# A diffusion block on one core: attention ordered by pair, two token tiles and head, and the modulation moved to ScalarE and GpSimd

## The chip, the core and the metric

The kernel runs on one core of a Trainium2 chip. A core has five engines that run on their own instruction queues, each in order: TensorE (PE in the profile, with PEld for its weight loads), VectorE (DVE), ScalarE (ACT), GpSimd (POOL) and SyncE (SP), which here issues every DMA. Matmul results land in PSUM, which has eight banks; everything else lives in SBUF. The metric is the device time of one execution in microseconds (us), lower is better. Three runs of the kernel before took 1487.81, 1483.56 and 1487.60 us, so the median is 1487.6 us.

## The reference, cut to what matters

One transformer block over 1024 tokens (a grid of 16 rows by 64 columns) of width 1024, in fp32, with 256 context tokens that are only attended to. Sixteen heads of 64.

```python
sh1, sc1, g1, sh2, sc2, g2 = adaln(c, w_mod, b_mod)            # silu(c) @ w_mod + b_mod, cut in six
csh1, csc1, *_ = adaln(c_ctx, w_mod, b_mod)
h  = rms_norm(x, norm1)   * (1 + sc1)  + sh1                    # 1024 x 1024
hc = rms_norm(ctx, norm1) * (1 + csc1) + csh1                   #  256 x 1024
q, k = rms_norm(heads(h @ w_q), q_gain), rms_norm(heads(h @ w_k), k_gain)   # norm over the 64 of a head
v = heads(h @ w_v);  kc = rms_norm(heads(hc @ w_k), k_gain);  vc = heads(hc @ w_v)
# each token attends to a window of 8 x 16 tokens (with a relative bias) and to all 256 context tokens
p = softmax([q @ k_window / 8 + rpb, q @ kc / 8])
x = x + g1 * ((p @ [v_window, vc]) @ w_o)
a, g = split(modulate(rms_norm(x, norm2), sh2, sc2) @ w_up)     # 1024 x 2816 each
x = x + g2 * ((a * gelu(dwconv3(g))) @ w_down)
```

`rms_norm(t) = t / sqrt(mean(t*t) + 1e-6) * gain`.

## The kernel before

Tokens are cut into eight tiles of 128 (each is 16 rows by 8 columns of the grid), t = 0 to 7, and the context into two, t = 8 and 9; the order of work is 8, 9, 0, 1, ... 7 (`TORD`). A window touches only the neighbouring tiles, so tile t attends to tiles t-1, t, t+1 and to the context: 512 scores a row at the edges (t = 0 and 7) and 640 elsewhere. Every fp32 product is made of three fp32r matmuls: an operand is split in a high part (`wh`, `hth`: a rounded copy made on ACT) and a low part (`wl`, `htl`: a subtraction on DVE or POOL).

The program has four stages:

1. **The prologue.** Shift and scale of the first norm from `w_mod` (tiles `mraw`); then each token tile `xt` is loaded, normalised, transposed on TensorE (`pt`), modulated and split (`hth`, `htl`). The loop interleaves this with the projections of the first pair of heads: after transposing tile number i it makes projections up to tile number i - `AHEAD`.
2. **The attention of eight pairs of heads.** `qkv_gen(p)` is the generator of the projections of pair p: ten tiles, 24 matmuls each into a PSUM tile `pq` (two buffers). When a tile's matmuls are done it is taken out of PSUM: ACT squares q and k (`qsq`), DVE sums the squares (`qss`, `L323`), DVE scales the sums and adds epsilon (`L324`), POOL takes the power of -1/2 (`L325`), and DVE writes `q` (per head), `kn` and the low part of `v` (per head; ACT writes its high part). `pq` is free again only after the last of these. `k_stack` transposes `kn` (`kt`) into the keys `k`. The steps (p, h, t) are: `stage_a` transposes q (`qt`, split into `qh`, `ql`); `stage_b` makes the scores `s` (one PSUM buffer of two banks), DVE adds the bias and finds the row's extreme (`L410`, writes `p`), ACT takes the exponential (`L412`), DVE the reciprocal of the sum (`m`, `L413`), POOL multiplies by it (`L417`); two steps later `stage_c` transposes `p` (`pl`, `pc`) and splits it (`pt`); three steps later `stage_d` multiplies by `v` (`po`), adds the two halves (ACT `ot`, DVE `or`) and stores to `o_dram`. The steps run over the head's eight tiles, then the other head's. Between the stages `filler(6)`, `filler(5)` and `filler(5)` put 16 matmuls of the projections of the *next* pair into each step; at step (h = 0, t = 5) what is left of one pair is emitted at once and the next pair's generator is started. `build_bias` makes one head's bias on POOL from `rpb`, at the end of the head before.
   Beside it `mod_gen` computes the remaining four parts of the modulation on DVE: 16 blocks of eight loads `mr` (128 x 256 each, two buffers), each multiplied by a column of `cs` and added to `macc` (`L469`, `L471`), one or two loads per step.
3. **The output projection.** `wo_first` makes its first half (pairs 0 to 3) beside the last pair; the second half, the second norm and the operands of the next product follow.
4. **The feed-forward part** in a Winograd form (seven products of halves in place of eight), up and down. The diff leaves its code alone.

What sets the order on each engine: the program is written in one order, and a scheduler of the compiler places each instruction when its inputs and a free buffer are there, the earlier-written first. The resulting queue of each engine is fixed at build time; at run time an engine that waits at its head holds up all that is queued behind it.

## Time and profile before

| | before |
|---|---|
| runs (three), median | 1483.56 to 1487.81 us, 1487.6 us |
| span of the profiled execution | 1491.8 us, the only time shown of that execution |
| mean granted TensorE clock | 0.974 of full speed |
| TensorE busy, 0 to 100 us (prologue) | 68.6 of 100 us |
| TensorE busy, 100 to 600 us (attention) | 479.2 of 500 us, clock 0.98 |
| DVE / ACT / POOL busy, 100 to 600 us | 418.3 / 295.1 / 259.6 us |
| TensorE busy, 830 to 1180 us (up projection) | 349.1 of 350 us |

The span runs from the first to the last instruction of one execution under the profiler. It is 4.2 us above the median of the runs. A matmul's span contains its way through the array, so consecutive matmuls overlap: TensorE's busy share is not its share of the peak, and a stall shows only where the spans do not touch. A row of the grouped view reads: line, engine, operation, tile written and tiles read, shapes, count, then busy us, mean ns of one, and the idle time of the engine before them with what ended it.

### The profile page before, as it was taken

The page shows a single profiled execution, that of the slowest core. Times are in us where ns is not written, and L with a number is a line of the kernel's source. Part 1 is how long each engine was busy: PE and PEld are TensorE (multiplying, and loading weights), DVE is VectorE, ACT ScalarE, POOL GpSimd, SP SyncE. Part 2 cuts the span into 40 slices and gives each one's busy share as a digit, 9 for nine tenths or more (in the row PEclk, how much of TensorE's full clock was granted, in tenths as well). Part 3 has the DMA queues.
Part 4 walks back from the last instruction along what each step waited for, and adds up shares of the span by engine and source line. Part 5 has one row for each costly group of instructions (what it writes and reads, how often), then busy time and mean ns, then how long its engine had stood idle before and what let it go on. Part 6 is the DMA issues. An engine that isn't in the chain of part 4 may idle for free.

```text
span 1491.8 us, 22077 instructions
## 1 busy us (share of the span) xinstructions
PE 1386.5 (93%) x7396; PEld 1200.0 (80%) x7396; DVE 1208.1 (81%) x2392; ACT 738.1 (49%) x1601; POOL 805.7 (54%) x672
## 2 busy tenths in 40 slices
PE   6689999999999999999996999999999987898998
PEld 2589889898989899888885777888888865686887
DVE  6778878888888878866589889788877779988884
ACT  6575645555565656645465434344343334244541
POOL 1455544545454546744368545555545568474872
PEclk9899999999999999999997999999999998899999
DMA  9612221313131202262132132233332347433343
GB/s 315 161 37 60 64 87 55 92 51 103 49 101 45 77 14 73 69 152 76 50 129 99 64 108 101 96 106 106 107 106 99 106 137 286 155 100 127 110 131 105
DMA packets 84827, 153.27 MB, mean 103 GB/s; under 512 B 9945, under 2 KB 49001, under 8 KB 84713
## 3 DMA queue, kind: packets, MB, share of 16 engines
q1 hardware_dynamic: 84712, 151.86, 32.7%
q8 instruction: 58, 0.95, 0.3%
q14 instruction: 57, 0.46, 0.1%
HBM read 119.05 MB, written 32.78 MB: 102 GB/s over the span
## 4 chain that ended last, share of the span: by engine, by line
PE 60%; DVE 20%; DMA 7%; POOL 5%; issue 4%; ACT 3%; SPq 0%; DVEq 0%; POOLq 0%; ACTq 0%
PE pg L740 8%; PE pa L740 7%; PE sw L740 6%; PE pq L301 5%; PE pq L303 5%; PE pq L305 5%; DMA mr<-in_w_mod_dram 2%; DVE y L787 2%; DVE p L410 2%; POOL u L688 2%; PE s L398 2%; PE po L448 2%; PE po L449 2%; PE py L525 2%; PE py L526 2%
## 5 line engine op out<-in xcount | busy, mean ns | idle before, releaser
L688 POOL TENSOR_TENSOR u<-ur,u 128x512 fp32r<-128x512 f32 x154 | 231.9, 1519 | 176.8 <-ACT u L687 175.1
L417 POOL TENSOR_TENSOR p<-p,m 128x640 f32<-128x640 f32 (+1 forms) x128 | 157.3, 1230 | 157.0 <-DVE m L413 116.0
L301 PE MATMUL pq<-wh,hth 128*128 128x384 f32 (+1 forms) x640 | 219.7, 343 | 17.1 <-DVE kn L340 15.3
L305 PE MATMUL pq<-wh,htl 128*128 128x384 f32 (+1 forms) x640 | 215.2, 336 | 2.4 <-DVE htl L194 1.4
L303 PE MATMUL pq<-wl,hth 128*128 128x384 f32 (+1 forms) x640 | 215.0, 336 | 0.5 <-POOL wl L147 0.5
L687 ACT ACTIVATE u<-ur 128x512 fp32r<-128x512 f32 x154 | 93.9, 628 | 116.1 <-PE sw L740 45.4
L412 ACT ACTIVATE p<-p,m 128x640 f32<-128x640 f32 (+1 forms) x128 | 102.9, 804 | 84.3 <-DVE m L410 75.2
L301 PEld LDWEIGHTS pq<-wh,hth 128*128 128x128 f32 x640 | 124.8, 195 | 23.1 <-DVE kn L340 9.2
L325 POOL TENSOR_TENSOR qss<-qss,mhalf 128x4 f32<-128x4 f32 (+1 forms) x80 | 79.9, 999 | 97.0 <-DVE qss L324 82.8
L305 PEld LDWEIGHTS pq<-wh,htl 128*128 128x128 f32 x640 | 124.7, 195 | 3.2 <-DVE htl L194 3.2
L303 PEld LDWEIGHTS pq<-wl,hth 128*128 128x128 f32 x640 | 124.8, 195 | 1.6 <-issue 0.9
L787 DVE SCALAR_TENSOR_TENSOR y<-g,cw,y 128x896 f32<-128x896 f32 (+1 forms) x132 | 102.8, 842 | 19.2 <-ACT y L781 19.1
L449 PE MATMUL po<-pt,v 128*128 128x256 f32 x352 | 93.3, 293 | 2.1 <-DVE pt L437 2.1
L448 PE MATMUL po<-pt,v 128*128 128x256 f32 x352 | 93.8, 289 | 0.1
L895 ACT ACTIVATE db<-dr 128x512 fp32r<-128x512 f32 x77 | 47.4, 629 | 87.3 <-PE dx L911 55.7
L871 POOL TENSOR_TENSOR da<-da 128x512 fp32r<-128x512 f32 x44 | 74.9, 1725 | 27.4 <-ACT da L870 27.4
L896 POOL TENSOR_TENSOR db<-dr,db 128x512 fp32r<-128x512 f32 x44 | 64.9, 1494 | 45.6 <-ACT db L895 34.3
L410 DVE CUSTOM_DVE_ANT_0 p<-s,bias 128x640 f32<-128x640 f32 x96 | 78.3, 816 | 9.5 <-PE s L399 8.9
L436 ACT ACTIVATE pt<-pl 128x384 fp32r<-128x384 f32 (+1 forms) x128 | 58.0, 461 | 47.6 <-PE pl L429 46.6
L471 DVE SCALAR_TENSOR_TENSOR macc<-mr,cs,macc 128x256 f32<-128x256 f32 x112 | 65.0, 581 | 13.9 <-DMA mr<-in_w_mod_dram 13.0
L437 DVE TENSOR_TENSOR pt<-pl,pt 128x384 fp32r<-128x384 f32 (+1 forms) x128 | 65.4, 516 | 6.7 <-ACT pt L436 6.2
L449 PEld LDWEIGHTS po<-pt,v 128*128 128x128 f32 x352 | 66.6, 189 | 4.0 <-DVE pt L437 3.4
(258 smaller groups left out, 4184.3 us busy)
## 6 DMA issues: line engine op xcount, KB each, us to landing
ur<-in_w_up_dram SPq DMA_DIRECT2D x44, 512.0 KB
da<-act_dram SPq DMA_DIRECT2D x77, 256.0 KB
mr<-in_w_mod_dram SPq DMA_DIRECT2D x128, 128.0 KB
dr<-in_w_down_dram SPq DMA_DIRECT2D x22, 512.0 KB
wraw<-in_w_qkv_dram SPq DMA_DIRECT2D x56, 192.0 KB
mraw<-in_w_mod_dram SPq DMA_DIRECT2D x16, 512.0 KB
act_dram<-sa SPq DMA_DIRECT2D x11, 512.0 KB
act_dram<-y SPq DMA_DIRECT2D x11, 512.0 KB
```

Source lines behind the costliest of these rows:

```text
L301: PE.matmul(pq[:, c0:], hth[t][:, k, :], wh[:, c0:], start=(k == 0), stop=False)
L303: PE.matmul(pq[:, c0:], hth[t][:, k, :], wl[:, c0:], start=False, stop=False)
L305: PE.matmul(pq[:, c0:], htl[t][:, k, :], wh[:, c0:], start=False, stop=(k == KC - 1))
L410: DVE.tensor_tensor_reduce(out=dst, in0=src, in1=bb, scale=1.0, scalar=3e38, op0=ALU.add, op1=ALU.min, accum_out=m[:, 0:1])
L412: ACT.activation(w[:, :n], w[:, :n], AF.Exp, bias=m[:, 0:1], scale=-1.0, accum_out=m[:, 1:2])
L417: POOL.tensor_tensor(w[:, :n], w[:, :n], m[:, 2:3].broadcast_to([P, n]), ALU.mult)
L448: PE.matmul(po, v, th[:, j].rearrange("p a b -> p (a b)"), start=(m == 0), stop=False)
L449: PE.matmul(po, v, tl[:, j].rearrange("p a b -> p (a b)"), start=False, stop=(m == len(blks) - 1))
L687: ACT.activation(s[:, 0], r[op], AF.Copy)
L688: POOL.tensor_tensor(s[:, 1], r[op], f(s[:, 0]), ALU.subtract)
L740: PE.matmul(bank, a, b, start=(start and k == 0 and n == 0), stop=(k == 3 and n == 2), skip_group_check=True)
L787: DVE.scalar_tensor_tensor(o, i, w, o, ALU.mult, ALU.add)
```

## The change

The change rewrites the attention's order and some of its small operations:

- **Steps by pair, two tiles, head.** The steps become (p, u, h, i) with t = 2u + i: two tiles of the first head, the same two of the second, then the next two tiles. The last pair takes u in the order 0, 2, 1, 3.
- **One chain of projections.** `work()` strings the projections of all eight pairs and the first half of the output projection into one generator. A counter `done` of finished tiles is capped at what the step needs plus five (`LEAD`), and `need()` emits what is missing.
- **Both heads in one operation.** `v` (high and low part), `q` and the bias tile now hold both heads; the buffers go from 23 half tiles to 10 tiles for `v` (`VB`) and from 14 to 6 for `q` (`QB`). For the second head the scores lie with the context behind the window instead of in front, so that both biases share the block of zeros.
- **Epsilon as a 65th column.** The squares are scaled by 1/64 on ACT and a constant 65th column holds epsilon, so the sum is the mean plus epsilon and `L324` is gone.
- **Modulation on ACT and POOL.** `L469` and `L471` become an ACT multiplication of every `mr` (`L481`) and, for seven of eight, an addition on POOL (`L483`).
- `AHEAD` goes from 1 to 3; `ot` is gone (ACT writes `or`, DVE adds in place).

```diff
-AHEAD = 1
+AHEAD = 3
+QB, VB, LEAD = 6, 10, 5
...
+    sqc = sb.tile([P, 4, DH + 1], F32, name="sqc")
+    POOL.memset(sqc[:, :, DH:], EPS)
...
-            ACT.activation(sq[:, 4 - n:, :], pq[:, c0:2 * P].rearrange("p (h d) -> p h d", d=DH), AF.Square)
-            DVE.tensor_reduce(ss[:, 4 - n:], sq[:, 4 - n:, :], axis=AX.X, op=ALU.add)
-            DVE.tensor_scalar(ss[:, 4 - n:], ss[:, 4 - n:], 1.0 / DH, EPS, ALU.mult, ALU.add)
+            ACT.activation(sqc[:, 4 - n:, :DH], pq[:, c0:2 * P].rearrange("p (h d) -> p h d", d=DH), AF.Square,
+                           scale=DH ** -0.5)
+            DVE.tensor_reduce(ss[:, 4 - n:], sqc[:, 4 - n:, :], axis=AX.X, op=ALU.add)
             POOL.tensor_tensor(ss[:, 4 - n:], ss[:, 4 - n:], mhalf[:, 4 - n:], ALU.pow)
-            for h in range(2):
-                v = sb.tile([P, 2, DH], F32R, tag="v", bufs=23, name=f"v{p}_{h}_{t}")
-                pv = pq[:, 2 * P + h * DH:2 * P + (h + 1) * DH]
-                ACT.activation(v[:, 0, :], pv, AF.Copy)
-                DVE.tensor_tensor(v[:, 1, :], pv, f(v[:, 0, :]), ALU.subtract)
...
+            v = sb.tile([P, 2, 2, DH], F32R, tag="v", bufs=VB, name=f"v{p}_{t}")
+            pv = pq[:, 2 * P:].rearrange("p (h d) -> p h d", d=DH)
+            ACT.activation(v[:, :, 0, :], pv, AF.Copy)
+            DVE.tensor_tensor(v[:, :, 1, :], pv, f(v[:, :, 0, :]), ALU.subtract)
...
+                q = sb.tile([P, 2, 2, DH], F32, tag="q", bufs=QB, name=f"q{p}_{t}")
+                DVE.tensor_tensor(q, pq[:, :P].rearrange("p (h d) -> p h d", d=DH).unsqueeze(2)
+                                  .broadcast_to([P, 2, 2, DH]),
+                                  ss[:, :2].unsqueeze(2).unsqueeze(3).broadcast_to([P, 2, 2, DH]), ALU.mult)
...
+            done[0] += 1
...
-        ACT.activation(tmp[a:b], po[o:o + DH], AF.Copy)
-        DVE.tensor_tensor(res[a:b], po[a:b], tmp[a:b], ALU.add)
+        ACT.activation(res[a:b], po[o:o + DH], AF.Copy)
+        DVE.tensor_tensor(res[a:b], po[a:b], res[a:b], ALU.add)
...
-                    if k == 0:
-                        DVE.tensor_scalar(acc, raw, cs[:, k, 0:1], None, ALU.mult)
-                    else:
-                        DVE.scalar_tensor_tensor(acc, raw, cs[:, k, 0:1], acc, ALU.mult, ALU.add)
+                    ACT.activation(acc if k == 0 else raw, raw, AF.Copy, scale=cs[:, k, 0:1])
+                    if k:
+                        POOL.tensor_tensor(acc, acc, raw, ALU.add)
...
-    steps = [(p, h, t) for p in range(NPAIR) for h in range(2) for t in range(NB)]
-    steps[-NB:] = [(NPAIR - 1, 1, t) for t in LORD]
+    steps = [(p, h, 2 * u + i) for p in range(NPAIR) for u in ((0, 1, 2, 3) if p + 1 < NPAIR else (0, 2, 1, 3))
+             for h in range(2) for i in range(2)]
...
+    def work():
+        for p in range(NPAIR):
+            yield from qkv_gen(p)
+        yield from wo_first()
...
-        while n > 0:
+        while n > 0 and done[0] < cap[0]:
...
-            if h == 0 and t == 5:
-                filler(10 ** 6)
-                fill = qkv_gen(p + 1) if p + 1 < NPAIR else wo_first()
+            cap[0] = 10 ** 6 if p + 1 == NPAIR else NT * p + 2 + 2 * (t // 2) + LEAD
+            need(p, t)
...
-            if si % NB == NB - 1 and 2 * p + h + 1 < HEADS:
-                build_bias(2 * p + h + 1)
+            if p + 1 < NPAIR and t == NB - 1:
+                build_bias(2 * (p + 1) + h)
```

What that moves in the queues, at three places. In the rows, the first number in a name is the pair, then the head where the tile belongs to one head, then the token tile; the last is a buffer number.

First, SP's queue in the prologue, from the first `rpb` on. `wraw` are weights of pair 1, `xt4` to `xt7` the last token tiles, `mr2048_0` and on the loads of the modulation. Before:

```order
L366 DMA rpb0_1109<-in_rpb_t_dram 128x384
L136 DMA wraw1_2_1140<-in_w_qkv_dram 128x384
L136 DMA wraw1_3_1142<-in_w_qkv_dram 128x384
L168 DMA xt4_532<-in_x_dram 128x1x1024
L136 DMA wraw1_4_1144<-in_w_qkv_dram 128x384
L467 DMA mr2048_0_1187<-in_w_mod_dram 128x256
L467 DMA mr2048_1_1251<-in_w_mod_dram 128x256
L168 DMA xt5_601<-in_x_dram 128x1x1024
L366 DMA rpb1_1498<-in_rpb_t_dram 128x384
L467 DMA mr2048_2_1254<-in_w_mod_dram 128x256
```

Now:

```order
L374 DMA rpb0_974<-in_rpb_t_dram 128x384
L480 DMA mr2048_0_1007<-in_w_mod_dram 128x256
L480 DMA mr2048_1_1028<-in_w_mod_dram 128x256
L169 DMA xt4_491<-in_x_dram 128x1x1024
L137 DMA wraw1_2_1313<-in_w_qkv_dram 128x384
L137 DMA wraw1_3_1315<-in_w_qkv_dram 128x384
L137 DMA wraw1_4_1317<-in_w_qkv_dram 128x384
L169 DMA xt5_522<-in_x_dram 128x1x1024
L480 DMA mr2048_2_1032<-in_w_mod_dram 128x256
L374 DMA rpb1_981<-in_rpb_t_dram 128x384
L480 DMA mr2048_3_1055<-in_w_mod_dram 128x256
L169 DMA xt6_591<-in_x_dram 128x1x1024
```

Before, `xt6` stands behind ten loads `mr`; now it stands behind four, with `xt7` right after it. The first two `mr` move ahead of `xt4` and of three `wraw`.

Second, TensorE between pairs 3 and 4, from the first score of pair 4 (`s4_0_0`) on. Before, the last projection of pair 4 (`pq4_7`) lies around the score, and the transposes `pl4_0_0` of that step come 64 rows after it, with 11 more matmuls of `pq4_7` and all 24 of the next tile between:

```order
L301 MATMUL pq4_7_5706<-wh4_4_4636,hth7_108 128x384
L398 MATMUL s4_0_0_5481<-k4_0_4826,qh4_0_0_5421 128x256
L399 MATMUL s4_0_0_5481<-k4_0_4826,qh4_0_0_5421 128x256
L398 MATMUL s4_0_0_5481<-k4_0_4826,ql4_0_0_5422 128x256
L399 MATMUL s4_0_0_5481<-k4_0_4826,ql4_0_0_5422 128x256
L303 MATMUL pq4_7_5706<-wl4_4_4637,hth7_108 128x384
L305 MATMUL pq4_7_5706<-wh4_4_4636,htl7_109 128x384
L429 MATMUL pl3_1_6_5498<-ident_60,p3_1_6_5326 128x128 x3
L301 MATMUL pq4_7_5706<-wh4_5_4663,hth7_108 128x384
```

Now no projection lies between `s4_0_0` and `pl4_0_0`: the rows are 11 transposes (`pl`, `pc`, `qt`) and 9 matmuls `po`. Its end, with the next projection behind it:

```order
L448 MATMUL pc3_1_3_5236<-ident_60,p3_1_7_5032 128x128 x2
L392 MATMUL qt4_1_0_5289<-ident_60,q4_0_5053 128x128
L392 MATMUL qt4_1_0_5289<-ident_60,q4_1_5089 128x128
L462 MATMUL po3_1_3_5332<-pt1_1_968,v3_5_4320 128x256
L463 MATMUL po3_1_3_5332<-pt1_1_971,v3_5_4320 128x256
L443 MATMUL pl3_1_7_5296<-ident_60,p3_1_7_5032 128x128 x2
L443 MATMUL pl4_0_0_5324<-ident_60,p4_0_0_5220 128x128 x2
L462 MATMUL po3_1_3_5332<-pt1_1_968,v3_6_4422 128x256
L362 MATMUL kt4_1_5183<-ident_60,kn4_1_5133 128x128
L308 MATMUL pq4_5_5272<-wh4_0_4537,hth5_104 128x384
```

The score and its transposes stand closer together. `pq4_5` waits for the PSUM buffer of `pq4_3`, and the `v` of that tile takes a buffer that the first two `po3_1_3` are the last to read.

Third, POOL in the same pair. Before:

```order
L371 TENSOR_TENSOR bias_396<-mr_394,rpb8_5411 128x128 x2
L417 TENSOR_TENSOR p3_1_0_4923<-p3_1_0_4923,m3_1_0_4924 128x512
L417 TENSOR_TENSOR p3_1_1_5001<-p3_1_1_5001,m3_1_1_5002 128x640
L325 TENSOR_TENSOR qss4_2_5244<-qss4_2_5244,mhalf_67 128x4
L325 TENSOR_TENSOR qss4_3_5337<-qss4_3_5337,mhalf_67 128x4
L417 TENSOR_TENSOR p3_1_2_5070<-p3_1_2_5070,m3_1_2_5071 128x640
```

Now:

```order
L430 TENSOR_TENSOR p3_1_4_4759<-p3_1_4_4759,m3_1_4_4760 128x640
L483 TENSOR_TENSOR macc4864_4746<-macc4864_4746,mr4864_4_4827 128x256
L483 TENSOR_TENSOR macc4864_4746<-macc4864_4746,mr4864_5_4831 128x256
L430 TENSOR_TENSOR p3_1_5_4804<-p3_1_5_4804,m3_1_5_4805 128x640
L483 TENSOR_TENSOR macc4864_4746<-macc4864_4746,mr4864_6_4888 128x256
L332 TENSOR_TENSOR qss4_1_5082<-qss4_1_5082,mhalf_67 128x4
L483 TENSOR_TENSOR macc4864_4746<-macc4864_4746,mr4864_7_4952 128x256
```

Between two normalisations (`p`) stand one or two additions of the modulation, and the power of a projection tile (`qss`) now has additions in front of it and behind it. On ACT the multiplications `mr` stand likewise between the exponentials and the copies.

More of the change, by code (lines that the diff above doesn't have):

```diff
@@ L277, in block_kernel @@
     SP.dma_start(out=mr, in_=mask_r)
-    bias = sb.tile([P, 5, 2 * P], F32, name="bias")
-    POOL.memset(bias[:, 0, :], 0.0)
+    bias = sb.tile([P, 16 * P], F32, name="bias")
+    BZ, BI, BE = 7 * P, (9 * P, 4 * P), ((12 * P, 14 * P), (0, 2 * P))
+    POOL.memset(bias[:, BZ:BZ + 2 * P], 0.0)
+    sqc = sb.tile([P, 4, DH + 1], F32, name="sqc")
+    POOL.memset(sqc[:, :, DH:], EPS)
     pth, ptl = [], []
@@ L546, in block_kernel @@
     mg = mod_gen()
-    fill = qkv_gen(0)
+    def work():
+        for p in range(NPAIR):
+            yield from qkv_gen(p)
+        yield from wo_first()
+    fill = work()
     stats_x(TORD[2])
@@ L555, in block_kernel @@
         if i >= AHEAD:
-            while (0, 1, TORD[i - AHEAD]) not in vt:
+            while (0, TORD[i - AHEAD]) not in vt:
                 next(fill)
@@ L565, in filler, with need @@
             n -= c
-    def need(p, h, t):
-        while (p, h, min(t + 1, NB - 1)) not in vt or (p, min(t + 1, NB - 1) // 2) not in kdone:
-            filler(1)
+    def need(p, t):
+        hi = min(t + 1, NB - 1)
+        while (p, hi) not in vt or (p, hi // 2) not in kdone:
+            next(fill)
+    cap = [LEAD]
     build_bias(0)
-    need(0, 0, 1)
+    build_bias(1)
+    need(0, 1)
     stage_a(0, 0, 0)
```

56 lines of the change are left out of this document (28 added, 28 removed).

## The prediction

> **What bounds the kernel now.** I read the page's head first, then the busy time by stage, then who waits for whom inside the attention, then single stalls in order of time.
>
> ```profile
> span 1491.8 us, 22077 instructions
> PE 1386.5 (93%) x7396; PEld 1200.0 (80%) x7396; DVE 1208.1 (81%) x2392; ACT 738.1 (49%) x1601; POOL 805.7 (54%) x672
> ```
>
> TensorE is busiest, but the share is an average. By stage (each row: stretch in us, its length, then busy us and count of PE, PEld, DVE, ACT, POOL, granted clock, DMA share, GB/s):
>
> ```profile
> 36.00:54.00 18.00, 11.64 (x78) 10.70 (x77) 15.65 (x37) 14.00 (x34) 12.66 (x17) 0.81 0.85 207
> 54.00:62.00 8.00, 0.81 (x4) 0.72 (x3) 5.28 (x14) 3.67 (x10) 2.10 (x3) 0.78 0.82 154
> 73.00:84.00 11.00, 6.18 (x41) 5.67 (x39) 7.75 (x25) 7.68 (x21) 4.42 (x6) 1.00 0.22 53
> 100.00:600.00 500.00, 479.17 (x3236) 461.96 (x3234) 418.29 (x1228) 295.14 (x779) 259.63 (x265) 0.98 0.23 68
> 600.00:700.00 100.00, 92.31 (x561) 84.70 (x561) 76.77 (x197) 55.85 (x130) 57.76 (x52) 0.97 0.38 101
> 750.00:830.00 80.00, 65.52 (x278) 51.90 (x277) 71.64 (x112) 47.09 (x118) 59.92 (x53) 0.87 0.29 99
> 830.00:1180.00 350.00, 349.07 (x1497) 280.64 (x1496) 287.84 (x342) 141.49 (x216) 185.38 (x126) 1.00 0.31 104
> ```
>
> The up projection (830 to 1180) has no idle TensorE and is untouched. The prologue loses 6.4, 7.2 and 4.8 us in the first three stretches; the attention loses 20.8 us in 500, plus a clock of 0.98. The attention is TensorE work with DVE close behind it. Where the modulation ends, this shows:
>
> ```profile
> 200.00:300.00 100.00, 94.90 (x632) 92.07 (x631) 83.15 (x244) 55.86 (x146) 48.65 (x50) 0.97 0.25 71
> 300.00:400.00 100.00, 95.19 (x646) 92.22 (x645) 86.08 (x257) 56.68 (x152) 47.90 (x50) 0.98 0.24 71
> 400.00:500.00 100.00, 96.28 (x644) 91.83 (x643) 86.46 (x249) 57.54 (x151) 49.86 (x51) 0.98 0.25 73
> 500.00:600.00 100.00, 97.56 (x685) 94.99 (x683) 78.37 (x234) 64.11 (x169) 59.39 (x61) 1.00 0.17 51
> ```
>
> The last row is the stretch without modulation: DVE is 7 points below the mean of the three, the clock is whole, and TensorE does 685 matmuls where the three rows before did 641 on average, at the same mix of work. So a busy DVE costs the attention about 7% of its pace. Who waits, from 100 to 600 us (total, times, longest):
>
> ```profile
> POOL p L417 <- DVE m L413: 78.4, 50, 6.2
> POOL qss L325 <- DVE qss L324: 70.3, 35, 6.3
> ACT p L412 <- DVE m L410: 61.9, 56, 2.9
> DVE macc L471 <- DMA mr<-in_w_mod_dram: 10.0, 22, 1.2
> PEld pq L301 <- DVE kn L340: 8.6, 15, 2.0
> ```
>
> ACT and POOL wait for DVE, and TensorE's own waits end with DVE's last read of a projection tile (`kn`).
>
> **The change part by part.** The rows that price it (the shape's own group where the mean would mix shapes):
>
> ```profile
> L471 DVE SCALAR_TENSOR_TENSOR macc<-mr,cs,macc 128x256 f32<-128x256 f32 x112 | 65.0, 581 | 13.9 <-DMA mr<-in_w_mod_dram 13.0
> L469 DVE TENSOR_SCALAR macc<-mr,cs 128x256 f32<-128x256 f32 x16 | 8.7, 543 | 1.6 <-DMA mr<-in_w_mod_dram 1.4 <-PE pmr L478 0.2
> L324 DVE TENSOR_SCALAR qss<-qss 128x4 f32<-128x4 f32 (+1 forms) x80 | 24.3, 303 | 0.4
> L334 DVE TENSOR_TENSOR q<-pq,qss 128x128 f32<-128x128 f32 x128 | 36.1, 282 | 8.9 <-POOL qss L325 8.7
> L330 DVE TENSOR_TENSOR v<-pq,v 128x64 fp32r<-128x64 f32 x160 | 34.6, 216 | 9.2 <-ACT v L329 8.4
> L646 ACT ACTIVATE b1h<-x 128x256 fp32r<-128x256 f32 x4 | 1.5, 422 | 0.0
> L647 POOL TENSOR_TENSOR b3l<-x,b3h x8: 716/831/1187, 762.9 to 812.7; 128x256 fp32r<-128x256 f32 x8
> L417 POOL TENSOR_TENSOR p<-p,m 128x640 f32<-128x640 f32 x96 | 122.6, 1278 | 143.3 <-DVE m L413 107.0 <-PE pc L434 8.8 <-DVE qss L324 6.3
> ```
>
> *DVE* loses 65.0 + 8.7 us of modulation and 24.3 us of `L324`. Its `v` goes from 160 of 128x64 (34.6 us) to 80 of 128x128, at 0.28 as `q` of that shape: 22.4 us, 12 saved. Its `q` goes from 128 of 128x128 (36.1 us) to 64 of 128x256; taken at 0.42 (ACT's copy of that shape; no DVE row has it from PSUM) 27 us, 9 saved. Together 119 us off DVE, against 1208.1.
>
> *ACT* gains 128 multiplications of 128x256 at 0.42 from the row of the same shape: 54 us; *POOL* gains 112 additions of that shape at 0.83, the median of its row: 93 us. Neither becomes the bound: spread over the 400 us with modulation, ACT goes to about 72 and POOL to about 73 us in 100. Their cover is the TensorE work of the attention; if it is gone, they show up in the chain below.
>
> The row on POOL is one price; the page "GPSIMD Engine Reference" of the Trainium skill (section Engine selection) speaks against this move: it gives elementwise work with two inputs to VectorE, being about twice as slow on GpSimd. By twice the 581 ns of `L471` the additions would cost 130 us, POOL would be at 82 us in 100, and the forecast would drift toward the slower rival. The trace's 831 ns is 1.4 times the DVE row, and decides.
>
> *What DVE's relief is worth.* At the modulation-free pace of the last stretch, the 400 us from 100 to 500 take 400 x 641/685 = 374: **26 us less**. It is not only the busy time. The next rows show one score's way (`s` ends at 319.85, DVE reads it at 321.30, ACT at 322.21, DVE's reciprocal not shown, POOL from 323.66 to 324.92), and what held DVE up: an addition of the modulation that took 1.25 us instead of 0.48, ending as POOL's `p` ended.
>
> ```profile
> 318.61 1.25 POOL L417 TENSOR_TENSOR p<-p,m 128x640 f32<-128x640 f32 x1 [1.96 <-DVE m L413]
> 318.90 1.25 DVE L471 SCALAR_TENSOR_TENSOR macc<-mr,cs,macc 128x256 f32<-128x256 f32 x1
> 319.57 0.28 PE L399 MATMUL s<-k,ql 128*128 128x256 f32 x1
> 319.69 0.49 PE L429 MATMUL pl<-ident,p 128*128 128x128 f32 x3
> 320.59 0.28 PE L448 MATMUL po<-pt,v 128*128 128x256 f32 x1
> 320.71 0.28 PE L449 MATMUL po<-pt,v 128*128 128x256 f32 x1
> 321.30 0.81 DVE L410 CUSTOM_DVE_ANT_0 p<-s,bias 128x640 f32<-128x640 f32 x1
> 322.21 0.83 ACT L412 ACTIVATE p<-p,m 128x640 f32<-128x640 f32 x1 [1.50 <-DVE m L410]
> 323.66 1.26 POOL L417 TENSOR_TENSOR p<-p,m 128x640 f32<-128x640 f32 x1
> ```
>
> `L324` and `L471` read and write SBUF alone, beside POOL; what stays on DVE in the loop reads PSUM. Less `v` and `q` on DVE is worth a little beyond the modulation: between 0 and the 21 us of DVE time that goes, I take 4, near the lower end, since from 500 us on only 2.4 us in 100 are idle.
>
> *What the order costs.* The step's way from `s` to the end of POOL's `p` took 5.1 us above; its four parts alone are 0.81 + 0.83 + 1.26 and about 0.4 for the two short ones, 3.3 us. Before, six microseconds or more of matmuls stand between a score and its transposes (transposes start every 0.11 us, `po` every 0.12). Now, between pairs, 11 transposes and 9 `po` stand there: 11 x 0.11 + 9 x 0.12 = 2.3 us. I find two more short places in each pair, with 3.7 and 4.0 us, since the ten `v` buffers keep projections out until `po` has read the old ones. If the way takes c, a pair loses 3c - 10. At 3.5 that is 1.2 us (the first place alone), at 5.1 it is 5.3; over the seven pairs 1 to 7, 8 and 37 us. I take 4.2, nearer the lower end, because DVE has less queued and a stalled TensorE gives the others nothing new: 2.6 a pair, **17 us more**.
>
> A stall also costs clock: after a stretch with a 2.8 us stall the next 3.4 us ran at half.
>
> ```profile
> 344.00:348.60 4.60, 1.87 (x14) 1.36 (x13) 4.60 (x14) 3.43 (x10) 3.47 (x4) 1.00 0.43 130
> 348.60:352.00 3.40, 3.40 (x17) 3.40 (x17) 2.49 (x7) 1.07 (x3) 1.13 (x1) 0.50 0.66 210
> ```
>
> The page "TensorE: Matmul & The Clock Gate" of the Trainium skill (section HAM oscillation) puts the line at idle gaps over some 3.4 us; here a shorter one was enough, so I follow the row. By the page the new short stalls (at most 2.8) never cost clock; by the row one a pair may cost 1.7, 12 us in all, which I leave to the range.
>
> *Prologue.* From 54 to 62 us TensorE waits for `pq`, whose readers stand on DVE behind an `mr` load. The first two `mr` are now loaded ahead of `xt4` and three `wraw`, and ACT, not DVE, waits for them. Later the last tokens wait behind ten `mr`, each waiting for its buffer:
>
> ```profile
> 57.76 11.69 SPq L467 DMA_DIRECT2D mr<-in_w_mod_dram x8
> 69.50 4.77 SPq L168 DMA_DIRECT2D xt<-in_x_dram x2
> 76.85 0.41 PE L301 MATMUL pq<-wh,hth 128*128 128x384 f32 x1 [3.16 <-DVE kn L340]
> ```
>
> Now `xt6` stands behind four. Between nothing and the 18.4 us that TensorE idles in the three stretches, I take half: **9 us less**. ACT pays: its copies of the tokens stand behind `mr` at the queue's head.
>
> *Tail.* With both heads' tiles 0, 1, 4, 5 finished first, the second half of the output projection mixes with the last steps. The 7.7 us idle in 600 to 700 bound the gain, 5 us of a badly placed `w_o` load the loss; I take **3 less**. The feed-forward rows keep their matmuls: 0, bounded by 2 either way. `ot`, the bias of two heads in one tile and the swapped scores take the same number of operations: 0, covered by ACT and POOL at 60 and 52% of the attention; without that cover, below 1 us a pair.
>
> Sum: -26 - 4 + 17 - 9 - 3 = **-25 us**. Against the profiled span that is 1466.8; the span lies 4.2 us above the runs' median, so against the median of 1487.6 it is **1463 us**.
>
> **The rivals.**
>
> *POOL takes DVE's place (slower).* Power and normalisation wait for an addition each: c becomes 5.1 + 0.83, about 5.9. Then the short places cost 3 x 5.9 - 10 = 7.7 a pair, 54 us, against gains of 42: **1499 us**. It decides from c = 5.4 on, where 7 x 6.2 eats the 42. For it speaks that one or two additions stand between any two `p` on POOL, and that both POOL and ACT now stand behind the DMA of `mr` (10.0 us on DVE before); against it the POOL waits above, 78.4 us for DVE alone.
>
> *A wash (no change).* The same at c of about 5.3, or the relief is worth half and c is 4.5: **1487 us**. For it: the relief is inferred from one stretch.
>
> *Most stalls go.* c is 3.5 (8 us), the prologue gives 15, the tail 8: -26 - 4 + 8 - 15 - 8 = -45, **1443 us**. For it: 3.3 us is the floor of the way. Against it: `v` must wait for `po`.
>
> **How the numbers follow.** About 0.3% (4.5 us) is what a measurement of this kernel can tell from no change. The forecast, 1448 to 1481, gets 0.51; most stalls gone 0.16; the wash 0.13; POOL in DVE's place 0.20. So faster 0.67, same 0.13, slower 0.20. The range leaves out a tail of each outer case: 1436 to 1498.
>
> **What would show it.** Right: in the attention DVE near 60 us in 100, POOL near 70, the clock at 0.99 or more, more than 660 matmuls per 100 us while the modulation runs, and stalls of 1 to 2 us at `pl` ended by POOL's `p`, one to three a pair. In the prologue less than 12 us idle from 36 to 84. Wrong: POOL's `p` or `qss` behind `macc` and TensorE waiting for them at every step; ACT's exponentials behind `mr` loads; or the first scores of a pair waiting for the bias.

## The result and the profile after

The changed kernel takes 1501.1 us (median of four runs, 1499.5 to 1502.8) against 1487.7 us before: a ratio of 1.0075 (95% interval 1.0053 to 1.0097). So it is about 11 us slower by the ratio and 13 by these medians, where 25 us less were forecast. Its profiled execution has a span of 1498.9 us, 7.1 more than that of before. The head of the page:

```profile
span 1498.9 us, 21970 instructions
PE 1391.6 (93%) x7396; PEld 1197.4 (80%) x7396; DVE 1134.0 (76%) x2040; ACT 785.3 (52%) x1649; POOL 871.0 (58%) x785
```

DVE lost 74 us, ACT gained 47 and POOL 65, where the prediction counted 119, 54 and 93. The rows that it priced on DVE did fall by 119 us in sum: the modulation and `L324` are gone, `v` went from 34.6 to 22.7 us and `q` from 36.1 to 26.8. The busy time fell less; in it, stretches in which neighbouring instructions overlap count once. The busy time by stage (stretch, its length, then busy us and count of PE, PEld, DVE, ACT, POOL, granted clock, DMA share, GB/s), of the changed kernel:

```profile
36.00:54.00 18.00, 11.26 (x74) 10.39 (x75) 16.00 (x37) 14.65 (x34) 13.13 (x16) 0.81 0.80 206
54.00:62.00 8.00, 6.34 (x35) 5.68 (x34) 7.22 (x20) 8.00 (x21) 6.16 (x10) 0.81 1.06 273
62.00:73.00 11.00, 8.52 (x53) 8.22 (x53) 8.91 (x21) 9.06 (x24) 8.07 (x13) 0.97 0.21 58
73.00:84.00 11.00, 11.00 (x61) 10.93 (x62) 7.95 (x19) 8.06 (x20) 9.39 (x13) 0.86 0.16 48
100.00:500.00 400.00, 383.31 (x2559) 363.55 (x2558) 269.69 (x736) 278.05 (x684) 269.01 (x310) 0.99 0.24 72
500.00:700.00 200.00, 182.83 (x1176) 171.47 (x1175) 140.03 (x346) 110.41 (x257) 105.72 (x99) 0.98 0.26 73
```

and the last two stretches of the kernel before:

```profile
100.00:500.00 400.00, 381.61 (x2553) 366.97 (x2552) 339.92 (x995) 231.02 (x610) 200.24 (x205) 0.98 0.25 72
500.00:700.00 200.00, 189.87 (x1244) 179.69 (x1243) 155.14 (x430) 119.96 (x299) 117.15 (x112) 0.98 0.27 76
```

Between 54 and 84 us TensorE idles 4 us instead of 12. Then, with the modulation running, DVE has gone from 85 to 67 us in 100, and TensorE does 2559 matmuls where it did 2553: what the relief bought, something else took. From 500 to 700 us it does 68 fewer. The waits from 100 to 600 us (total, times, longest) of the changed kernel, a selection:

```profile
POOL p L430 <- DVE m L426: 55.5, 39, 10.3
ACT mr L481 <- DMA mr<-in_w_mod_dram: 46.0, 59, 2.1
POOL macc L483 <- ACT mr L481: 27.2, 37, 2.9
ACT p L425 <- DVE m L423: 22.2, 26, 2.0
PE po L462 <- DVE or L468: 7.9, 8, 2.1
PE s L410 <- DVE m L423: 2.8, 8, 0.5
PE pl L443 <- DVE pt L454: 2.4, 6, 0.4
PE qt L392 <- DVE pt L451: 1.8, 3, 0.9
PE pc L448 <- POOL p L430: 0.8, 1, 0.8
PE pl L443 <- POOL p L430: 0.3, 1, 0.3
```

ACT now waits 46 us for loads of `mr`; before, DVE waited 10. TensorE's own waits end mostly with DVE's `or` and `pt`, the second half of emptying a PSUM tile whose first half ACT does, then with DVE's read of the scores (`m`), and hardly ever with POOL's `p`. Waits of this kind were there before, beside those for `kn`; the kernel before had, in the same 500 us:

```profile
PE kt L354 <- DVE pt L440: 6.8, 3, 2.7
```

One of the changed kernel's, between pairs 2 and 3, in order of time (start, us, engine, line; idle time before it in brackets; rows of other work are left out):

```profile
317.40 0.49 PE L443 MATMUL pl<-ident,p 128*128 128x128 f32 x3
317.40 0.51 ACT L481 ACTIVATE mr<-mr,cs 128x256 f32<-128x256 f32 x1 [1.93 <-DMA mr<-in_w_mod_dram]
317.82 0.36 ACT L450 ACTIVATE pt<-pl 128x256 fp32r<-128x256 f32 x1
318.21 0.42 DVE L451 TENSOR_TENSOR pt<-pl,pt 128x256 fp32r<-128x256 f32 x1 [2.23 <-ACT pt L450]
319.15 0.51 ACT L481 ACTIVATE mr<-mr,cs 128x256 f32<-128x256 f32 x1 [0.97 <-DMA mr<-in_w_mod_dram]
319.83 0.48 ACT L450 ACTIVATE pt<-pl 128x384 fp32r<-128x384 f32 x1
320.34 0.56 DVE L451 TENSOR_TENSOR pt<-pl,pt 128x384 fp32r<-128x384 f32 x1
320.96 0.44 PE L392 MATMUL qt<-ident,q 128*128 128x128 f32 x2 [0.78 <-DVE pt L451]
320.97 0.51 ACT L481 ACTIVATE mr<-mr,cs 128x256 f32<-128x256 f32 x1 [0.66 <-DMA mr<-in_w_mod_dram]
321.39 0.70 ACT L425 ACTIVATE p<-p,m 128x512 f32<-128x512 f32 x1
322.21 0.38 ACT L467 ACTIVATE or<-po 64x256 f32<-64x256 f32 x1
322.62 0.42 DVE L468 TENSOR_TENSOR or<-po,or 64x256 f32<-64x256 f32 x1 [0.24 <-ACT or L467]
323.09 0.39 PE L462 MATMUL po<-pt,v 128*128 128x256 f32 x1 [1.70 <-DVE or L468]
```

Three times in four microseconds ACT stands still for a load (1.93 + 0.97 + 0.66 us) with `pt` and `or` queued behind it; DVE waits for ACT, and TensorE, which has no projection between these transposes, waits for DVE. This is one example; how much of all the stalls it stands for, the experiments have to say.

For all kernels below I worked out TensorE's idle time from its trace: the span less what each matmul takes when the next one follows at once (0.231 us for 512 columns, 0.174 for 384, 0.118 for 256, 0.108 for 128, the usual spacing in these traces; about 1326 us in every kernel). Time in which the granted clock was half, and matmuls stood further apart, counts as idle too. It is cut where 100, 500 and 640 us of that work are done. The columns hold the prologue with the start of pair 0; the pairs up to the middle of pair 6; the rest of the attention with the last pair ("the last pair" below); and all that follows. These are single profiles, and the spacings are rounded, which moves all kernels alike by 1 or 2 us. The changed kernel, g1, h2 and h3 have the same code up to the last pair; between them the prologue's column moves by 4 us and the pairs' by 2. The columns of a kernel belong to its profiled execution, which need not be the median one.

| kernel | ratio of the runs | prologue, to 100 | pairs, 100 to 500 | last pair, 500 to 640 | behind it |
|---|---|---|---|---|---|
| before | 1 | 44.3 | 41.2 | 15.2 | 65.2 |
| changed | 1.0075 | 38.4 | 40.3 | 22.7 | 71.0 |
| e1 changed, modulation on DVE | 1.0155 | 40.4 | 49.4 | 24.3 | 70.7 |
| e2 before, modulation on ACT and POOL | 0.9941 | 41.5 | 28.5 | 17.9 | 65.9 |
| e3 before, without modulation | 0.9972 | 49.2 | 26.5 | 19.5 | 66.0 |
| e4 changed, without modulation | 0.9957 | 40.9 | 25.8 | 22.6 | 71.7 |
| f1 all but the order | 0.9892 | 41.5 | 24.2 | 18.5 | 65.3 |
| f2 changed, no loads of `mr` | 0.9968 | 37.4 | 29.9 | 22.3 | 71.6 |
| h2 changed, no loads of `w_o` | 1.0070 | 38.9 | 41.2 | 9.8 | 84.2 |
| h3 changed, last pair by heads | 1.0063 | 42.8 | 42.4 | 25.0 | 66.9 |
| h4 changed, LEAD 8 | 1.0123 | 43.6 | 53.2 | 16.9 | 70.8 |
| i2 changed, buffer for the product | 1.0089 | 36.8 | 33.8 | 22.1 | 77.9 |

### The profile page after: what moved, and what is told of

Its sections match the earlier page's. It is cut to its first block, busy times and chain, and to the rows that moved or that the text cites. A ratio compares the mean times of both kernels' runs of the same rounds, so it can differ in the third digit from the quotient of the medians.

```text
span 1498.9 us, 21970 instructions
## 1 busy us (share of the span) xinstructions
PE 1391.6 (93%) x7396; PEld 1197.4 (80%) x7396; DVE 1134.0 (76%) x2040; ACT 785.3 (52%) x1649; POOL 871.0 (58%) x785
## 5 line engine op out<-in xcount | busy, mean ns | idle before, releaser
L805 DVE SCALAR_TENSOR_TENSOR y<-g,cw,y 128x896 f32<-128x896 f32 (+1 forms) x132 | 110.9, 905 | 18.0 <-ACT y L799 18.0
L483 POOL TENSOR_TENSOR macc<-macc,mr 128x256 f32<-128x256 f32 x112 | 83.1, 742 | 37.9 <-ACT mr L481 27.2
L889 POOL TENSOR_TENSOR da<-da 128x512 fp32r<-128x512 f32 x44 | 68.0, 1569 | 39.3 <-ACT da L888 20.3
L451 DVE TENSOR_TENSOR pt<-pl,pt 128x384 fp32r<-128x384 f32 (+1 forms) x128 | 65.4, 518 | 26.3 <-ACT pt L450 25.8
L481 ACT ACTIVATE mr<-mr,cs 128x256 f32<-128x256 f32 x112 | 57.0, 509 | 51.4 <-DMA mr<-in_w_mod_dram 46.6
```

What stands on the lines that cost most here:

```text
L483: POOL.tensor_tensor(acc, acc, raw, ALU.add)
L805: DVE.scalar_tensor_tensor(o, i, w, o, ALU.mult, ALU.add)
```

## The experiments

### What the modulation costs, and where (e1 to e4)

e1 puts back the two DVE lines in the changed kernel, e2 puts the ACT and POOL lines into the kernel before:

```diff
-                    ACT.activation(acc if k == 0 else raw, raw, AF.Copy, scale=cs[:, k, 0:1])
-                    if k:
-                        POOL.tensor_tensor(acc, acc, raw, ALU.add)
+                    if k == 0:
+                        DVE.tensor_scalar(acc, raw, cs[:, k, 0:1], None, ALU.mult)
+                    else:
+                        DVE.scalar_tensor_tensor(acc, raw, cs[:, k, 0:1], acc, ALU.mult, ALU.add)
```

e3 (before) and e4 (changed) keep all loads and only the product of k = 0.

> The changed kernel with the modulation put back on DVE (the two DVE lines of before, everything else as changed). Theory A (the relief of DVE is worth its 26 us in any order of steps, and the new order costs about 30 to 40): about 1525, slower than the changed kernel's 1501 by 20 or more. Theory B (what the modulation frees on DVE it takes back on ACT and POOL, above all by ACT waiting 46 us for the loads of mr at the head of its queue): 1495 to 1503, no worse than the changed kernel.

> The kernel before with the modulation alone moved to ACT and POOL. Theory A: about 1462 to 1468, the 26 us of the prediction's first term nearly whole. Theory B: 1484 to 1495, nothing gained.

> The kernel before with seven of eight products of the modulation left out (all loads of mr stay, each eighth one is still multiplied on DVE), so the output's gates and the second norm's modulation are not the reference's. It gives the whole price of the modulation on DVE in the old order. Theory A and B alike: 1458 to 1466 (the pace of 685 matmuls in 100 us throughout). Theory C (the pace of the stretch from 500 us has another cause than the missing modulation): 1480 to 1488.

> The changed kernel with seven of eight products of the modulation left out (loads stay, each eighth one multiplied on ACT). It gives the price of the modulation on ACT and POOL in the new order. Theory A (the new order alone costs 30 to 40): 1490 to 1500, little below the changed kernel. Theory B (ACT and POOL pay for it): 1470 to 1480.

Measured: e1 1.0155 (1.0124 to 1.0185), e2 0.9941 (0.9921 to 0.9961), e3 0.9972 (0.9959 to 0.9985), e4 0.9957 (0.9940 to 0.9975). Neither A nor B: moving the modulation is worth 0.6% in the old order (9 us) and 0.8% in the new (12 us), the right sign at less than half of 26. e3 says why. Its row:

```profile
100.00:500.00 400.00, 388.95 (x2654) 378.48 (x2652) 303.95 (x933) 244.07 (x647) 208.62 (x220) 0.98 0.24 73
```

Without the modulation the old order does 2654 matmuls in these 400 us, not 4 x 685 = 2740; by its ratio this is what theory C expected. The same work as before would take 400 x 2553/2654 = 385 us: the whole of the modulation was worth 15 us of pace, and over the run 4 (by the table the prologue and the last pair lost 5 and 4 again). The stretch from 500 us that the prediction took for the modulation-free pace was a good one, and its matmuls were lighter: weighed by the spacings above, the four stretches hold 88.9, 90.2, 90.4 and 94.9 us of matmul work, which would have given some 22 us and not 26. e2, which computes the modulation, came out faster over the run than e3, which leaves most of it out; by the table the two differ in the prologue, not in the pairs.

The table's column for the pairs holds the second finding:

| pairs, idle us | no modulation | on ACT and POOL | on DVE |
|---|---|---|---|
| old order | 26.5 | 28.5 | 41.2 |
| new order | 25.8 | 40.3 | 49.4 |

Without modulation the new order costs nothing there. The modulation on ACT and POOL costs 2 us in the old order and 14.5 in the new, though ACT waits about as long for the loads. e2's row of that wait:

```profile
ACT mr L468 <- DMA mr<-in_w_mod_dram: 42.4, 48, 3.2
```

### All but the order (f1)

The kernel before with the ACT and POOL lines, the 65th column, ACT writing `or`, and `AHEAD = 3`; steps, generators, `v`, `q` and `bias` as before.

> The kernel before with everything of the change that does not need the new order: modulation on ACT and POOL, epsilon as a 65th column, ACT writing `or`, AHEAD = 3. Steps, chain of projections, v, q and bias per head stay as before. Theory D (the new order and the merged buffers are what lost the time, since they make short places without projections): ratio to before 0.985 to 0.992, 20 us or more below the changed kernel's 1.0075. Rival E (one of the small parts costs the time): 1.000 or more.

Measured: 0.9892 (0.9857 to 0.9928), 1475.8 us against 1491.1 on that chip. So 1.8% (27 us) lie in the order of steps, the one chain and the merged buffers together. By the table: 16 us in the pairs, 4 in the last pair, 6 behind it, less 3 in the prologue, 23 in all. Theory D's range held. Against e2 the pairs lose another 4 us of idle time, with the 65th column, `or` and `AHEAD` together; `v` and `q` are still per head here. The three parts of the order were not undone one by one, and no run gives the new order more `v` buffers. So what the ten buffers cost, which the prediction named, is not known.

### Loads that an engine waits for (f2, f3, f4, g2, h1, i1, i2)

f2 leaves the loads out; ACT multiplies the identity instead:

```diff
-                    SP.dma_start(out=raw, in_=wm[:, k, s0:s0 + MW])
-                    ACT.activation(acc if k == 0 else raw, raw, AF.Copy, scale=cs[:, k, 0:1])
+                    ACT.activation((acc if k == 0 else raw).rearrange("p (a b) -> p a b", b=P),
+                                   ident.unsqueeze(1).broadcast_to([P, 2, P]), AF.Copy, scale=cs[:, k, 0:1])
```

> The changed kernel with the loads of mr left out: ACT multiplies the identity (same shape) instead, POOL adds as before, so the modulation's result is not the reference's. Takes away ACT's 46 us of waiting for those loads and 17 MB of traffic, and nothing else. Theory D1 (ACT waiting for mr at the head of its queue is what makes the short places between pairs long): ratio 0.996 to 1.000, most of the 17 us that leaving the products out gave. Theory D2 (the work on ACT and POOL itself is the cost, not the wait): 1.004 to 1.007.

Measured: 0.9968 (0.9953 to 0.9984), 16 us less than the changed kernel, nearly all that leaving out the products gave (e4). e4 keeps the loads without the work, f2 the work without the loads, and both gain about the same. So the price lies in the two together: work that waits for loads, or work beside their traffic. The stalls only become shorter: `or` still ends 6.0 us of TensorE's waits from 100 to 600 us, against 7.9. Six runs tried to tell the wait from the traffic or to shorten the wait.

f3 keeps the modulation out of a pair's first four steps:

```diff
-        next(mg, None)
-        if si % 4:
+        if si % 16 >= 4:
+            next(mg, None)
             next(mg, None)
```

> The changed kernel with no modulation in the first four steps of each pair and two blocks' loads a step in the other twelve (24 per pair, 28 before). The loads, ACT multiplications and POOL additions leave the short places between pairs, all else stays. Theory D (short places and modulation together cost it): the stalls at the pair boundaries go from 5 us to about 2.5, ratio 1.000 to 1.003. Rival (the modulation costs the same wherever it stands): 1.006 to 1.009.

Measured: 1.0076 (1.0050 to 1.0102), as the rival said: ACT still waited 38.4 us from 100 to 600 us, and the pairs' idle time stayed at 40.4.

f4 gives `mr` a third buffer (`bufs=3`); g2 also writes each load two turns ahead of its multiplication. To make room, both load the convolution's constants `cw` and `cb` only behind the attention, as h1, i2 and g4 do below:

> The changed kernel with three buffers for mr instead of two (the convolution's small constants are loaded later to make room). Loads run one further ahead. Theory D1 (ACT's wait for mr): that wait falls from 46 us to under 25 and the ratio to 1.000 to 1.004. Theory D2: the wait falls, the ratio stays at 1.006 to 1.009.

> The changed kernel with three buffers for mr and each load written two turns before its multiplication (three buffers alone left ACT's wait at 38 us). Theory D1: ACT's wait falls under 15 us and the ratio to 0.998 to 1.002, close to 0.9968 without the loads. Rival D3 (the gain without loads came from the traffic taken away, not from the wait): the wait falls, the ratio stays at 1.005 or above.

Measured: f4 1.0083 (1.0051 to 1.0116), g2 1.0093 (1.0057 to 1.0129). The waits of f4 and g2:

```profile
ACT mr L477 <- DMA mr<-in_w_mod_dram: 38.3, 54, 2.2
```

```profile
ACT mr L488 <- DMA mr<-in_w_mod_dram: 40.1, 51, 2.3
```

They fell by 6 to 8 us of 46, too little to tell D1 from its rivals. In f4 the pairs idle some 6 us less than in the changed kernel, and what follows the last pair 4 more. A free buffer or an earlier load lets the compiler's order put the multiplication earlier too; that this is the reason is argued, not shown.

h1 and i1 keep the loads but let nobody read them, with ACT on the identity as in f2:

```diff
+                    lost = sb.tile([P, MW], F32, tag="lost", bufs=1, name=f"ml{s0}_{k}")      # h1
+                    lost = dram.tile([P, MW], F32, tag="lost", bufs=2, name=f"ml{s0}_{k}")    # i1
+                    SP.dma_start(out=lost, in_=wm[:, k, s0:s0 + MW])
```

> The changed kernel with all loads of mr kept but read by nobody (a buffer of their own), while ACT multiplies the identity of the same shape and POOL adds as before; the modulation's result is not the reference's. Traffic and work are those of the changed kernel, only the wait is gone. Theory D1 (the wait is the cost): 0.995 to 0.999, as without the loads (0.9968). Rival D3 (traffic beside work is the cost): 1.004 to 1.009.

> The changed kernel with each load of mr going to one of two tiles in DRAM that nobody reads, while ACT multiplies the identity of the same shape and POOL adds as before; the modulation's result is not the reference's. The reads from HBM, the issues on SP's queue and the work on ACT and POOL stay, the wait of ACT is gone (writes to DRAM are new). Theory D1 (the wait is the cost): 0.995 to 0.999, as without the loads (0.9968). Rival D3 (traffic beside work is the cost): 1.004 to 1.009.

Measured: h1 1.0386 (1.0359 to 1.0413), i1 1.0061 (1.0046 to 1.0076). Both missed what they were made for. In h1 each load waited in SP's queue for the one before (203 us in 121 turns, from 36 to 330 us), and the loads behind them came late (100 to 330 us):

```profile
ACT wh L147 <- DMA wraw<-in_w_qkv_dram: 29.8, 5, 10.5
POOL bias L376 <- DMA rpb<-in_rpb_t_dram: 23.7, 4, 13.3
```

In i1 nothing held the loads back, and they ran early, beside the prologue; its stages:

```profile
36.00:200.00 164.00, 142.60 (x884) 135.35 (x885) 111.02 (x286) 111.00 (x273) 104.16 (x128) 0.91 0.56 155
200.00:500.00 300.00, 292.16 (x2004) 280.53 (x2003) 210.13 (x572) 215.87 (x528) 209.57 (x244) 1.00 0.12 34
```

Its prologue idles 50.6 us against 38.4, its pairs 27.1 against 40.3: the gain of f2 is there, lost again in front, but the traffic (34 GB/s against 70 in the changed kernel) was no longer beside the pairs.

i2 computes everything, with a buffer for the product, so that the next multiplication waits for POOL's addition instead of a load:

```diff
-                    ACT.activation(acc if k == 0 else raw, raw, AF.Copy, scale=cs[:, k, 0:1])
+                    pr = sb.tile([P, MW], F32, tag="mprod", bufs=1, name=f"mq{s0}_{k}") if k else acc
+                    ACT.activation(pr, raw, AF.Copy, scale=cs[:, k, 0:1])
```

> The changed kernel with ACT's product in one buffer of its own, so that an mr is free for its next load as soon as ACT has read it, and ACT's next multiplication waits for POOL's addition, not for a load. Everything is computed. Theory D1: ACT's wait for loads falls from 46 to under 20 us and the ratio to 0.998 to 1.003, if the new wait for POOL does not take its place; if it does, ACT's total wait for loads and additions stays near 46 us and the ratio at 1.005 or above. Rival D3: the wait falls and the ratio stays at 1.005 or above.

Measured: 1.0089 (1.0065 to 1.0113). The wait went down, and half of what went came back as the other wait:

```profile
ACT mq L478 <- POOL macc L480: 17.7, 25, 2.4
ACT mq L478 <- DMA mr<-in_w_mod_dram: 11.6, 12, 1.7
```

The pairs idle 33.8 us instead of 40.3, but what follows the last pair 77.9 instead of 71.0. So a shorter wait of ACT goes with shorter stalls in the pairs, and the run is no faster for it. That does not show the shorter wait to be worthless, since i2 is not clean: all five kernels that load `cw` and `cb` later idle more behind the last pair than the kernel they start from (f4, h1 and, against f1, g4 by about 4 us, i2 by 7, g2 by 12). Why is not shown; for f4 and i2 it eats most or all of what the pairs gain. Whether the wait, or traffic beside work, is the cost of f2's 16 us is not settled: the stalls in the trace speak for the wait, and no run here decides.

### The last pair and what follows (g1, h2, h3)

g1 writes each load of `w_o` one turn ahead, h2 leaves these loads out (the gate times itself takes their place), h3 changes the last pair's steps:

```diff
+    steps[-12:] = [(NPAIR - 1, 0, t) for t in range(2, NB)] + [(NPAIR - 1, 1, t) for t in (4, 5, 2, 3, 6, 7)]
```

> The changed kernel with each load of w_o (wor) written one turn before the work on it, where it now stands right in front of it. In the last pair DVE, POOL and ACT wait 2 to 9 us for these loads at the head of their queues, and TensorE's stalls of 2 us there end with work queued behind. Theory F (a load that an engine waits for becomes TensorE's stall where no projections lie between): the last pair's 23 us of idle time fall to 12 to 16 and the ratio goes from 1.0075 to 1.001 to 1.004. Rival G (the last pair's cost is its order of tiles, whatever the loads do): 1.006 to 1.009.

> The changed kernel without the eight loads of w_o: the gate is multiplied by itself instead, so the output projection is not the reference's; all work on DVE, POOL and ACT stays. Takes away the waits for wor in the last pair. Theory F (these waits are the last pair's stalls): idle there from 23 to 12 to 16 us, ratio 1.001 to 1.004. Rival G (its order of steps): 1.006 to 1.009, idle 20 or more.

> The changed kernel with the last pair's steps by head, nearly as before (tiles 0 and 1 of both heads, then head 0, then head 1; two q tiles take the buffers that mr no longer uses). Rival G (the order is what the last pair loses): 1.001 to 1.004. Theory F: 1.006 to 1.009.

Measured: g1 1.0073 (1.0052 to 1.0095), with POOL still waiting 22.1 us for `wor` between 560 and 760 us, so it tells nothing; h2 1.0070 (1.0048 to 1.0091); h3 1.0063 (1.0039 to 1.0087). h2 is the instructive one. Its stages, and those of the changed kernel below:

```profile
590.00:700.00 110.00, 104.29 (x612) 93.91 (x612) 78.68 (x180) 55.87 (x123) 57.37 (x50) 1.00 0.28 73
750.00:830.00 80.00, 57.85 (x229) 43.90 (x228) 71.55 (x104) 47.87 (x121) 57.95 (x52) 0.83 0.26 90
```

```profile
590.00:700.00 110.00, 94.75 (x556) 85.54 (x555) 74.05 (x169) 53.58 (x119) 56.51 (x48) 0.97 0.35 93
750.00:830.00 80.00, 62.33 (x280) 48.62 (x279) 68.78 (x113) 48.20 (x123) 54.19 (x51) 0.87 0.25 86
```

Theory F was right about the stalls (idle in the last pair 9.8 us instead of 22.7) and wrong about the time: 13 us came back behind it. About 7 of them came back in the second norm, where DVE is at 86 to 89 us in 100 and TensorE at 72 to 78: what TensorE does earlier there, it waits longer for the norm's elementwise work. The rest came in the feed-forward part, mostly at the end of the up projection, and no run explains it. h3 took 4 us from behind the last pair and gave 2 to it: with the runs' interval, no difference shown. The 6 us behind the last pair stand in every kernel of the new order in the table but h3, with or without modulation (70.7 to 71.7 in e1, e4 and f2; more in h2 and i2), and in none of the old (65.2 to 66.0); h3 (66.9) points to the last pair's steps.

### Two numbers (g3, h4) and a better version (g4)

> The changed kernel with AHEAD = 1 as before: the prologue's part alone is undone. By the traces the prologue of the changed kernel is 6 us shorter. If AHEAD = 3 is what did it, the ratio goes from 1.0075 to 1.010 to 1.013; if it was the loads of mr that no longer stand in front of the tokens, or chance, it stays at 1.006 to 1.009.

Measured: 1.0125 (1.0098 to 1.0152). `AHEAD = 3` is worth 0.5%, some 7 us, in the new order: without it the prologue idles 42.1 us instead of 38.4 and the pairs 46.8 instead of 40.3. The first difference is no larger than what the prologue moves by itself (42.8 in h3), and in the old order f1 with `AHEAD = 3` and e2 without idle alike there, 41.5 us. So where the 7 us lie is not shown.

> The changed kernel with LEAD = 8 instead of 5. By the order of instructions the matmuls that are missing between scores and their transposes (against 5 us) fall from 31 to 24 us over pairs 1 to 7, and a projection's PSUM buffer is wanted back less often within 6 us (deficit 18 to 8 us). If the short places count as the prediction says: 5 to 8 us less, ratio 1.002 to 1.005. If the stalls come from waits for loads alone: 1.006 to 1.009.

Measured: 1.0123 (1.0105 to 1.0142), slower where 5 to 8 us less were expected. The last pair idles 6 us less, but the first six pairs 13 more and the prologue 5 more (h3 has 4 of these without the change). Counting matmuls between a score and its transposes in the order did not give the price of these places.

> The old order with all small parts of the change (f1, ratio 0.9892) and both kinds of loads, mr (three buffers) and w_o, written ahead as in the two kernels above. If the loads cost only where no projections lie between, f1 gains little: 0.984 to 0.990, the gain coming from its last pair, where TensorE once stalls 5 us. If they cost everywhere: 0.978 to 0.983.

Measured: 0.9889 (0.9874 to 0.9904), 1475.7 us, the same as f1. In the old order writing the loads ahead gains nothing, with the later load of `cw` and `cb` in it. f1 and g4 beat both kernels, the one before by 16 us and the changed one by some 27.

## Why the prediction was wrong

**The modulation's relief: −26, measured −9 to −13.** This step failed. It divided one stretch's pace (685) by three others' (641) and called the difference the modulation. The mix of work was not the same, which is 4 of the 26. e3 has the pace without the modulation in the same place: 2654 in 400 us, 15 us and not 26. Moving it is worth 9 us over the run in the old order (e2) and 12 in the new (e1); in the pairs' column 13 and 9. The rows of one score's way did not bear the term either: the long addition ended 0.3 us after POOL's `p`, and three more operations of DVE stood between it and the read of the score. Its cover was right in kind: ACT came to 70 us in 100 and POOL to 67, and neither became the bound. What it left out is that ACT inherits the wait for the loads, at 46 us instead of 10.

**`v` and `q` on DVE: −4, not measured.** They became cheaper as priced (21 us in sum), but no run has them without the new order. What f1 gains against e2, 4 us in the pairs, comes from other parts: `L324`, to which the sum gave nothing of its own, `or` and `AHEAD`.

**Short places: +17, measured +16** in the pairs (changed against f1, so with the one chain and the merged buffers). The size was right by luck, since the mechanism was another. The term priced the way from a score to POOL's `p`, at c = 4.2 (seven times 2.6 is 18, not 17). That way came to 4.8 us (mean over all 128 steps from the end of `s` to the end of POOL's `p`; 5.2 before), from which the formula would have made 31. TensorE's waits there end mostly with `or`, `pt` and the read of the scores: PSUM tiles that are not yet emptied. In the prediction's rows of before TensorE waited for `kn` alone; the wait for `pt`, about as long, was left out. 10 of the 16 go when the loads go (f2). That ACT standing in front of a load holds these tiles up is seen in single stalls and argued for the sum. The clock that the new stalls might cost, up to 12 us left to the range, did not come: it was granted at 0.99 from 100 to 500 us, and at 0.98 before.

**Prologue: −9, measured −6** in the profile, with 10.9 us idle from 36 to 84 us where less than 12 were asked. Right in kind; the column moves by 4 by itself. g3 gives `AHEAD` 7 us over the run, so the term named the loads of `mr` and not `AHEAD`; which of the two shortened the prologue is not shown.

**Tail: −3, measured +8 in the last pair and +6 behind it** (against before; +4 and +6 against f1). This step failed with the wrong sign. It took the idle time of one stretch for a bound of the gain. It named a badly placed load of `w_o` as a loss of up to 5 us, but h2 shows these waits to be worth 13 us of idle time in the last pair. And it did not see that the second norm behind is not bound by TensorE; for the 6 us there h3 points to the last pair's steps.

By the table's columns the sum is −13 (e2) − 4 (f1) + 16 − 6 + 13 = +6, against +7 in the profiled spans; it has to close, since the columns are parts of the spans. The runs say +11. The rival that named 1499 us had the time and not the mechanism: POOL's `p` ended two stalls, 1.1 us together, from 100 to 600 us. Of the signs that were to show the prediction right, DVE came to 67 in 100 and not 60, POOL to 67 and the clock to 0.99, and the matmuls stayed at 640 in 100 us where more than 660 were asked. The wrong signs that were named included ACT's exponentials behind `mr` loads. That one comes near to what happened: behind these loads stand also the copies `pt` and `or`, which TensorE waits for.

## What to carry to other kernels

Price a relief from the same stretch of a run without the work, or from the spread of several stretches; one good stretch is no rate. When a step that reads freshly loaded data moves to another engine, its wait for the load moves too, and what it costs depends on what stands behind it in that queue: the same work on ACT and POOL, with ACT waiting 42 to 46 us, cost 2 us of TensorE time in the old order and 14 in the new, which leaves places without projections between a score and its transposes. And look at every edit that was only meant to make room: here the later load of two small constants went with 4 us or more at another place. And before counting a gain near the end of a stage, look whether the next stage is bound by the same engine: of 13 us that TensorE no longer waited in the last pair, about 7 were waited for in the norm behind it, and the rest later.

## What was not expected of the hardware

The two moved operations, in the changed kernel's groups:

```profile
L483 POOL TENSOR_TENSOR macc<-macc,mr 128x256 f32<-128x256 f32 x112 | 83.1, 742 | 37.9 <-ACT mr L481 27.2
L481 ACT ACTIVATE mr<-mr,cs 128x256 f32<-128x256 f32 x112 | 57.0, 509 | 51.4 <-DMA mr<-in_w_mod_dram 46.6
```

POOL's addition took 0.74 us, less than the 0.83 that was assumed and 1.3 times DVE's 0.58. That is not like for like: DVE's operation multiplied as well, and its mean holds some of up to 1.36 us. The same subtraction of 128x256 on both engines, `b1l` on DVE and `b3l` on POOL, takes 0.41 and 0.72 us at its fastest in the changed kernel, 1.8 times; so the prediction's 1.4 understates the gap. ACT's multiplication by a column took 0.51 us instead of 0.42, the duration of its plain copy of that shape. Each of ACT's 59 waits for a load was 0.8 us on average, and stayed at 0.7 to 0.8 with a third buffer (38.3 us, 54 times) and with loads written two turns ahead (40.1 us, 51 times). And 128 loads that nobody reads, into one buffer, made a kernel 46 us slower than the changed one; the waits above put this down to what stood behind them in SP's queue.
